# Projecting q and k as one group of seven half-size products, with sums of tokens and of weights

## The chip, the cores and the metric

The kernel runs on one core of one Trainium2 chip. The metric is the device time of one execution in microseconds (us), lower being better. Of the kernel before, three runs are shown: 1118.29 us in the median, 1117.27 to 1118.49.

## What is computed

Two layers of an encoder over 256 tokens of width 1024. Each layer has a feed-forward stage (SwiGLU of width 2816), a mixing stage, and a second feed-forward stage, with an RMS norm ahead of and behind each. The change is in the mixing stage, whose input is projected to five things:

```python
h = rms_norm(x, mix_pre_g[l])
u_pool, q_da, k_da, v_da, q_ca = jnp.split(h @ w_in[l], IN_SPLITS, axis=-1)   # 256, 512, 512, 512, 256 columns
...
q = apply_partial_rope(q_da.reshape(B, S, DA_HEADS, 2, DA_HEAD_DIM), cos, sin)
k = apply_partial_rope(k_da.reshape(B, S, DA_HEADS, 2, DA_HEAD_DIM), cos, sin)
...
kv = rms_norm(mem, mem_norm_g[l]) @ w_mem_kv[l]
...
merged = g_pool * (y_pool @ w_br_pool[l]) + g_da * (y_da @ w_br_da[l]) + g_ca * (y_ca @ w_br_ca[l])
x = x + rms_norm(merged @ w_out[l], mix_post_g[l])
```

Differential attention uses q, k and v; cross-attention uses q_ca and the keys and values that are made of 256 memory tokens; a pooling branch uses u_pool; three gates of 1024 columns each weigh the branches.

## The kernel before

**Numbers in two parts.** TensorE (PE) multiplies numbers of a reduced f32 kind. To keep precision, each operand is split into a high part (a cast on ScalarE, ACT: L119 for weights, L164 and L175 for tokens) and a low part (what is left, on VectorE, DVE: L120, L165, L176). Each product of two tiles is then three matmuls, high by high, high by low and low by high (`mm3`, L229).

**Weights.** They come packed in units of 128x2048 (`_pack`, L924), each 1 MB, in the order of use. `load_unit` (L100) loads a unit into one of five `raw` buffers; `split_unit` (L113) makes `wh` and `wl` of it, in halves of 1024 columns or, for the first five units of a stage, in quarters of 512; `wts` has five buffers of each. So loading and splitting run ahead of PE by as many units as there are buffers.

**Tokens.** The normed tokens lie turned (channels on partitions) as a pair of high and low parts, `xhl` in the profile: `xt_pair` (L170), two buffers used in turn. `pre_norm` (L187) makes them at the end of the stage ahead: it norms one half of the tokens (128 of them; index c) on DVE and ACT, turns it on PE (L207) and splits it. The turns of the second half are issued only after a given number of matmuls of the next stage (`T_UP`, by `issue_after`), so that PE has other work while the norm runs.

**The mixing stage** (`mix`, L596). Four units hold the weights of q (512 columns, upper and lower half of the 1024 input channels) and of k. For each token half c, `form_b2` (L264) makes q and then k, 24 matmuls of 512 columns each, so 96 in all; ACT copies them out of PSUM (L623), DVE rotates 16 columns of each head (L627 to L630), PE turns the result (L634) and ACT copies that (L635). Then follow v (two units, 48 matmuls), the pooled channels and q of the cross-attention (one unit each, `form_a`, 48 matmuls of 256 columns each), the memory's keys and values (48 matmuls), and the gates (288 matmuls). The scores, softmaxes and their products are strewn among these: `fill` lists the matmuls from v on, and `place(at)` issues a step after matmul number `at` of the list (`T_KT`, `T_DA`, `T_PV`, `T_SC`, `T_LN`, `T_CA`, `T_CAV`).

**Memory tokens.** `mem_gain` (L578) loads the memory's tokens in the feed-forward stage ahead (L583), and the mixing stage scales and splits them behind q and k (L637, by L175 and L176).

**Groups that are there already.** In the second feed-forward stage of both layers and the first of layer 1, three pairs of up-projection tiles are made as a group (`group`, L384): a product of 256 tokens, 1024 channels and 1024 columns in seven products of half the size each way, by a scheme of Strassen's kind. DVE makes sums of weight tiles in place on the raw units (L366, 128x2048), sums of token tiles once per stage (`token_sums`, L374, from plain copies that `pre_norm` keeps, L212), and adds the products up (L366, 128x512). `PLAN` puts downs and ups between the groups.

Which instruction stands where on an engine is set by a scheduler that lists the program engine by engine; `issue_after` adds an order by hand. Each engine takes its own list strictly in that order.

Of the kernel before, what the change touches and what calls it, by code (L numbers as in the profile page):

```python
# [9 lines left out]
F32 = mybir.dt.float32  # L10
# [24 lines left out]
T_ROPE = 13  # L35
# [5 lines left out]
T_KT = (200, 222)  # L41
# [10 lines left out]
def encoder_kernel(ctx, tc, x_d, xt_d, mem_d, memt_d, pos_d, w_d, gains_d, cols_d, lamv_d, poolw_d, cst_d, out_d):  # L52
# [6 lines left out]
    xts = ctx.enter_context(tc.tile_pool(name="xts", bufs=2))  # L59
# [110 lines left out]
    def xt_pair():  # L170
        t = xts.tile([P, 2, 2, KT, P], F32R, name="xhl")
        return t[:, 0], t[:, 1], t.rearrange("p s c k t -> p (s c) k t")
# [93 lines left out]

    def rows_chunk(c, banks, todo, lhs_of, first, last):
        done = []
        for b in range(2):
            fs = slice(b * 512, (b + 1) * 512)  # L270
            for (w, kk) in todo:
                wh = w[0].rearrange("p (k m) -> p k m", k=2)
                wl = w[1].rearrange("p (k m) -> p k m", k=2)
                for k in range(2):
                    ah, al = lhs_of(c, kk, k)
                    for i, (a, ww) in enumerate(((ah, wh), (ah, wl), (al, wh))):
                        done.append(nc.tensor.matmul(  # L277
                            out=banks[b], lhsT=a, rhs=ww[:, k, fs],
                            start=(kk == first and k == 0 and i == 0),
                            stop=(kk == last and k == 1 and i == 2),  # L280
                        ))
        return done
# [14 lines left out]
    def ffn(i, xx, late, kept, g_post, finish, ahead, raw_rstd=None):  # L297
# [53 lines left out]
        def up_both(p):  # L351
            ws = (next_unit(), next_unit())
            for c in range(2):
                up(p, c, ws, leave=1 - c)
                if kept and p == 2 and c == 0:
                    token_sums()

        def product(out, at, w, first=True, last=True):
            wv = [t.rearrange("p (k m) -> p k m", k=4) for t in w]
            return mm3(out, [(at(k), (wv[0][:, k, :], wv[1][:, k, :])) for k in range(4)], first, last)  # L360

        def tokens(c, b):
            return lambda k: (xx[0][:, c, 4 * b + k, :], xx[1][:, c, 4 * b + k, :])

        def add(out, a, b):
            nc.vector.tensor_tensor(out=out, in0=a, in1=b, op=ALU.add)  # L366

        if kept:
            sums = xts.tile([P, 2, 4 * 4, P], F32R, name="xhl")

            def summed(j):
                return lambda k: (sums[:, 0, 4 * j + k, :], sums[:, 1, 4 * j + k, :])

        def token_sums():  # L374
            a11, a12, a21, a22 = (kept[c, b] for c in range(2) for b in range(2))
            s1 = t2()
            nc.vector.tensor_tensor(out=s1, in0=a22, in1=a21, op=ALU.subtract)
            nc.vector.tensor_tensor(out=a21, in0=a11, in1=a21, op=ALU.subtract)
            nc.vector.scalar_tensor_tensor(out=a11, in0=s1, scalar=-1.0, in1=a11, op0=ALU.mult, op1=ALU.subtract)
            nc.vector.scalar_tensor_tensor(out=a12, in0=a11, scalar=-1.0, in1=a12, op0=ALU.mult, op1=ALU.subtract)  # L380
            for j, t in enumerate((s1, a11, a21, a12)):
                split(t.rearrange("p (k t) -> p k t", t=P), sums[:, 0, 4 * j:4 * j + 4, :], sums[:, 1, 4 * j:4 * j + 4, :])
# [195 lines left out]
    def mem_gain(l):  # L578
        mm = xt_pair()
        loaded = []  # L580
        for b in range(4):
            t = hids.tile([P, 2, 2, P], F32, name="hid")
            nc.sync.dma_start(out=t, in_=memt_d[:, b * 512:(b + 1) * 512].rearrange("p (k c t) -> p k c t", k=2, c=2))  # L583
            loaded.append(t)

        def scaled():
            for b, t in enumerate(loaded):
                for i in range(2):
                    k = 2 * b + i
                    col = 3 * DEPTH + KT + KT * l + k  # L590
                    gained_split((mm[0][:, :, k, :], mm[1][:, :, k, :]), t[:, i], colt[:, col:col + 1])
            return mm

        return scaled

    def mix(l, xx, late, mm, finish):  # L596
# [4 lines left out]
        qkT = wts.tile([P, 2, 2, HEADS, P], F32, name="wh")  # L601
        qT, kT = qkT[:, 0], qkT[:, 1]
# [3 lines left out]
        kc = kv[:, 1536:2048].rearrange("p (t s) -> p t s", t=2)  # L606
        held = rawp.tile([P, 2048], F32, name="raw")
        vc, up, pooled, pw = (held[:, a:b].rearrange("p (t s) -> p t s", t=2) for a, b in ((0, 512), (512, 1056), (1056, 1568), (1568, 1824)))
        nc.sync.dma_start(out=pw, in_=poolw_d[l])

        ws = [next_unit() for _ in range(4)]
        done, wait = [], []
        for c in range(2):
            qk = s4.tile([P, D], F32, name="s4")
            for p in range(2):
                ps = ma_bank()
                now = form_b2(ps, ws[2 * p], ws[2 * p + 1], c, xx)
                done += now
                if c == 0 and p == 1:
                    issue_after(late, done[T_UP])  # L620
                issue_after(wait, now[T_ROPE])
                wait = []
                nc.scalar.copy(out=qk[:, p * 512:(p + 1) * 512], in_=ps)  # L623
            g = qk.rearrange("p (g d) -> p g d", d=64)
# [6 lines left out]
            for dst, off in ((qT, 0), (kT, 512)):  # L631
                tp = mb_bank()
                for h in range(HEADS):
                    wait.append(nc.tensor.transpose(out=tp[:, h * P:(h + 1) * P], in_=qk[:, off + h * P:off + (h + 1) * P], identity=ident))  # L634
                nc.scalar.copy(out=dst[:, c], in_=tp.rearrange("p (h t) -> p h t", h=HEADS))  # L635

        mm = mm()  # L637
        ws = [next_unit() for _ in range(2)]
        fill, placed = [], []

        def place(at):
            placed.append((at, []))
            return placed[-1][1]

        for c in range(2):
            ps = ma_bank()
            now = form_b2(ps, ws[0], ws[1], c, xx)
            fill += now
            issue_after(wait, now[T_ROPE])
            wait = []  # L650
            nc.scalar.copy(out=v[:, c, :], in_=ps)

        w = next_unit()
# [78 lines left out]
        yh, yl, _ = xt_pair()  # L732
# [75 lines left out]
        mg = xt_pair()  # L808
# [45 lines left out]
    cur = xt_pair()  # L854
# [18 lines left out]
    for i, (kind, l, row) in enumerate(stages):  # L873
        nx = {}

        def finish(c):
# [5 lines left out]
            if c == 0:  # L882
                nx["xx"] = xt_pair()
                nx["kept"] = {} if stages[i + 1][0] == "ffn" else None
# [3 lines left out]
        if kind == "ffn":  # L888
            def ahead():
# [3 lines left out]
                if row == 0:  # L893
                    nx["mem"] = mem_gain(l)

            late = ffn(i, cur, late, kept, gain(l * 10 + row + 1), finish, ahead, [rst[:, c:c + 1] for c in range(2)] if i == 0 else None)
        else:
            late = mix(l, cur, late, mem, finish)
        cur, mem, kept = nx.get("xx"), nx.get("mem"), nx.get("kept")
# [24 lines left out]
def _pack(a, np):  # L924
# [34 lines left out]
    for l in range(L):  # L959
        ffn(a["ffn1_w_up"][l], a["ffn1_w_down"][l], l == 0)  # L960
        wi = a["w_in"][l]
        for s in (256, 768, 1280):
            wide(wi, slice(s, s + 512))
# [53 lines left out]
```

## Time and profile before

| | |
|---|---|
| median of 3 runs | 1118.29 us |
| the profiled execution, whole | 1117.58 us |
| its span, from the first to the last instruction | 1115.3 us |
| PE busy | 1106.0 us (99%) |
| DVE busy | 892.5 us (80%) |
| ACT busy | 652.0 us (58%) |
| granted PE clock, mean | 0.999 |

The profile gives busy time by engine, groups of instructions by line and shape (count, busy time, mean of one), what each engine waited for, and instructions in order of time from the span's start. The first mixing stage's q starts at 194.57 us, that of layer 1 at 741.47. A matmul's listed duration overlaps its neighbours'; what one costs in a row of many is the distance from start to start.

### The profile page before, as it was taken

The numbers are of one execution on the slowest core, as the hardware profiler recorded it, in microseconds if no ns is written. First come the engines' busy times: TensorE is split into PE (matmuls) and PEld (weight loads), VectorE is DVE, ScalarE is ACT, GpSimd is POOL, SyncE is SP. The second block draws the span as 40 slices with busy tenths as digits, with TensorE's granted clock in tenths as the row PEclk, the third lists the DMA queues.
The fourth block names the chain that finished last, engine by engine and source line by source line (L and its number), as shares of the span: only waits on it lengthen the run. The fifth ranks groups of instructions, "written<-read, shape, count | busy, mean of one in ns | idle before, by whom it ended". The sixth has DMA issues, their size and how long they took to land.

```text
span 1115.3 us, 13906 instructions
## 1 busy us (share of the span) xinstructions
PE 1106.0 (99%) x5247; PEld 912.4 (82%) x5247; DVE 892.5 (80%) x1215; ACT 652.0 (58%) x1082; POOL 25.0 (2%) x37
## 2 busy tenths in 40 slices
PE   9999999999999999999999999999999999999997
PEld 6888888888888888888888888888888888888886
DVE  6765556757857899999989999996676678999994
ACT  7656345646575557474675574765566647575571
POOL 0000000000000100000000000010000001000000
PEclk9999999999999999999999999999999999999999
DMA  9966543564563453563951736575445644273731
GB/s 343 385 239 227 214 150 130 189 227 144 198 218 139 173 205 132 209 244 135 332 199 71 302 118 221 201 269 196 170 172 191 236 158 175 89 254 138 286 114 38
DMA packets 35489, 218.27 MB, mean 196 GB/s; under 512 B 4192, under 2 KB 4448, under 8 KB 11232
## 3 DMA queue, kind: packets, MB, share of 16 engines
q1 hardware_dynamic: 35424, 217.40, 53.6%
q8 instruction: 41, 0.67, 0.2%
q14 instruction: 24, 0.20, 0.0%
HBM read 216.33 MB, written 1.05 MB: 195 GB/s over the span
## 4 chain that ended last, share of the span: by engine, by line
PE 97%; DMA 1%; ACT 1%; DVE 0%; POOL 0%; issue 0%; SPq 0%; DVEq 0%; POOLq 0%; ACTq 0%
PE ma L235 52%; PE acc L277 26%; PE mb L235 9%; PE acc L235 5%; PE mb L325 2%; PE mb L207 1%; PE acc L672 1%; PE acc L695 1%; PE mb L564 1%; DMA hid<-in_xt 1%; PE acc L758 1%; DMA raw<-in_w 0%; PE acc L742 0%; PE mb L831 0%; PE mb L634 0%; ACT wh L119 0%
## 5 line engine op out<-in xcount | busy, mean ns | idle before, releaser
L120 DVE TENSOR_TENSOR wl<-raw,wh 128x1024 fp32r<-128x1024 f32 (+1 forms) x498 | 524.5, 1093 | 99.2 <-ACT wh L119 96.8
L119 ACT CAST wh<-raw 128x1024 fp32r<-128x1024 f32 (+1 forms) x498 | 445.0, 949 | 198.0 <-DVE raw L366 62.1
L235 PE MATMUL ma<-wh,xhl 128*128 128x512 f32 x1664 | 529.8, 393 | 0.7 <-ACT wh L119 0.7
L235 PEld LDWEIGHTS ma<-wh,xhl 128*128 128x128 f32 x1664 | 311.5, 188 | 66.3 <-ACT wh L119 1.8
L235 PE MATMUL ma<-wl,xhl 128*128 128x512 f32 x832 | 327.0, 393 | 0.2 <-DVE wl L120 0.2
L277 PE MATMUL acc<-wh,hid 128*128 128x512 f32 x704 | 228.1, 395 | 0.0
L235 PEld LDWEIGHTS ma<-wl,xhl 128*128 128x128 f32 x832 | 156.4, 188 | 32.7 <-issue 1.0
L277 PEld LDWEIGHTS acc<-wh,hid 128*128 128x128 f32 x704 | 132.2, 188 | 27.0
L277 PE MATMUL acc<-wl,hid 128*128 128x512 f32 x352 | 136.7, 390 | 0.0
L235 PE MATMUL mb<-wh,xhl 128*128 128x512 f32 x280 | 90.4, 389 | 0.0
L366 DVE TENSOR_TENSOR raw<-raw 128x2048 f32<-128x2048 f32 x36 | 82.4, 2288 | 0.4
L277 PEld LDWEIGHTS acc<-wl,hid 128*128 128x128 f32 x352 | 66.3, 188 | 12.6
L235 PEld LDWEIGHTS mb<-wh,xhl 128*128 128x128 f32 x280 | 52.6, 188 | 10.9
L235 PE MATMUL mb<-wl,xhl 128*128 128x512 f32 x140 | 54.5, 389 | 0.0
L235 PE MATMUL acc<-wh,xhl 128*128 128x512 f32 x160 | 51.6, 391 | 0.0
L340 ACT ACTIVATE s<-ma 128x256 f32<-128x256 f32 x24 | 8.9, 386 | 64.6 <-PE ma L235 64.3
L148 POOL TENSOR_TENSOR sm<-sm,mhalf 128x1 f32<-128x1 f32 (+1 forms) x26 | 22.0, 846 | 1002.0 <-DVE sm L157 822.8
L155 ACT ACTIVATE junk<-acc 128x512 bf16<-128x512 f32 x24 | 14.4, 599 | 48.0 <-PE acc L277 48.0
L277 PE MATMUL acc<-wh,xhl 128*128 128x512 f32 x128 | 40.7, 394 | 0.0
L164 ACT CAST hid<-mb 128x256 fp32r<-128x256 f32 x88 | 32.1, 370 | 13.1 <-PE mb L325 10.3
L165 DVE TENSOR_TENSOR hid<-mb,hid 128x256 fp32r<-128x256 f32 x88 | 36.6, 419 | 1.6 <-ACT hid L164 1.4
L235 PEld LDWEIGHTS acc<-wh,xhl 128*128 128x128 f32 x160 | 30.0, 188 | 6.1
(161 smaller groups left out, 882.7 us busy)
## 6 DMA issues: line engine op xcount, KB each, us to landing
raw<-in_w SPq DMA_DIRECT2D x189, 1024.0 KB, 4.8
gain<-in_gains SPq DMA_DIRECT2D x17, 512.0 KB, 4.2
raw<-in_w SPq DMA_DIRECT2D x8, 256.0 KB, 5.6
hid<-in_memt SPq DMA_DIRECT2D x8, 256.0 KB, 7.5
hid<-in_xt SPq DMA_DIRECT2D x4, 256.0 KB, 5.3
raw<-in_w SPq DMA_DIRECT2D x2, 512.0 KB, 7.3
x<-in_x SPq DMA_DIRECT2D x4, 256.0 KB, 6.6
hid<-in_mem SPq DMA_DIRECT2D x4, 256.0 KB, 7.5
```

The source lines that it names most:

```text
L119: high = nc.scalar.copy(out=h[:, cs], in_=raw[:, cs])
L120: low = nc.vector.tensor_tensor(out=l[:, cs], in0=raw[:, cs], in1=h.bitcast(F32)[:, cs], op=ALU.subtract)
L148: nc.gpsimd.tensor_tensor(out=r, in0=v, in1=mhalf[:, :n], op=ALU.pow)
L155: sq.append(nc.scalar.activation(out=junk, in_=h, func=AF.Square, scale=fold / 32.0, accum_out=s[:, i:i + 1]))
L164: high = nc.scalar.copy(out=h, in_=ps)
L165: return high, nc.vector.tensor_tensor(out=l, in0=ps, in1=h.bitcast(F32), op=ALU.subtract)
L207: tps.append(nc.tensor.transpose(out=ps[:, k * P:(k + 1) * P], in_=xn[:, i * P:(i + 1) * P], identity=ident))
L235: done.append(nc.tensor.matmul(out=out, lhsT=lhsT, rhs=rhs, start=(first and i == 0), stop=(last and i == n - 1)))
L277: done.append(nc.tensor.matmul(out=banks[b], lhsT=a, rhs=ww[:, k, fs], start=(kk == first and k == 0 and i == 0), stop=(kk == last and k = ...
L325: nc.tensor.transpose(out=tp[:, u * P:(u + 1) * P], in_=hn[:, u * P:(u + 1) * P], identity=ident)
L366: nc.vector.tensor_tensor(out=out, in0=a, in1=b, op=ALU.add)
L564: ins.append(nc.tensor.transpose(out=tp[:, i * P:(i + 1) * P], in_=a[:, hh, kt * P:(kt + 1) * P], identity=ident))
```

## The change

q and k are made as one group. The weights of q and k are four raw units: w11 and w12 (upper half of the channels; columns of q, columns of k), w22 and w21 (lower half; k, q). The group's seven products are, in the order of the code: pa (w11), pe (w21), pd (w11+w12), pb (w11+w12+w22), pc (w12+w22), pf (w22) and pg (w21+w11+w12+w22), each 12 matmuls of 512 columns; pd, pb, pc and pf take sums of tokens. v comes first: its first token half ahead of the group, its second between pe and pd. The rotation, the turns and their copies follow behind the group, among the matmuls of the pooled channels and of q_ca (`T_ROPE` is now a pair of places in `fill`). The memory's tokens are loaded and split behind that too, in the mixing stage, no longer ahead of it. `fill` loses v's 48 matmuls, and `T_KT` is lowered by 48; the other places keep their numbers. The token pairs have two named buffers, `xa` and `xb`, in place of `xhl`. `pre_norm` keeps plain copies of the tokens ahead of every stage now (four more copies on ACT per mixing stage).

```diff
-T_ROPE = 13
+T_ROPE = (13, 40)
-T_KT = (200, 222)
+T_KT = (152, 174)
...
-        ws = [next_unit() for _ in range(4)]
-        done, wait = [], []
-        for c in range(2):
-            qk = s4.tile([P, D], F32, name="s4")
-            for p in range(2):
-                ps = ma_bank()
-                now = form_b2(ps, ws[2 * p], ws[2 * p + 1], c, xx)
...
+        ws = [next_unit() for _ in range(2)]
+        done = v_half(0)
+        w11, w12, w22, w21 = (next_raw() for _ in range(4))
+        pa, pe = ma_bank(), ma_bank()
+        done += product(pa, tokens_of(xx, 0, 0), split_unit(w11, 2))
+        nc.scalar.copy(out=u2, in_=pa)
+        done += product(pe, tokens_of(xx, 0, 1), split_unit(w21, 2))
+        add(s, u2, pe)
+        issue_after(late, done[T_UP])
+        token_sums(kept, sums)
+        v_half(1)
+        add(w11, w11, w12)
+        pd = mb_bank()
+        product(pd, summed(0), split_unit(w11, 2))
+        add(w11, w11, w22)
+        add(w12, w12, w22)
+        pb = mb_bank()
+        product(pb, summed(1), split_unit(w11, 2))
+        add(u2, u2, pb)
+        add(w21, w21, w11)
+        pc = ma_bank()
+        product(pc, summed(2), split_unit(w12, 2))
+        add(u3, u2, pc)
+        add(u2, u2, pd)
+        add(v1, u3, pd)
+        pf = mb_bank()
+        product(pf, summed(3), split_unit(w22, 2))
+        add(u2, u2, pf)
+        pg = ma_bank()
+        product(pg, tokens_of(xx, 1, 1), split_unit(w21, 2))
...
+            if c == 1:
+                add(u3, u3, pg)
...
+        mm = mem_gain(l, 1 - slot)
...
-                nx["kept"] = {} if stages[i + 1][0] == "ffn" else None
+                nx["kept"] = {}
...
-        for s in (256, 768, 1280):
-            wide(wi, slice(s, s + 512))
+        wide(wi, slice(1280, 1792))
+        for half, col in ((0, 256), (0, 768), (1, 768), (1, 256)):
+            block(wi, half, col)
```

`product` makes 12 matmuls (four channel tiles, three each), `add` is one DVE addition, `token_sums` four DVE operations of 128x512 and four splits (a cast on ACT, a subtraction on DVE). In the changed kernel's lines, additions are L275, splits still L119, L120, L164 and L165, turns of q and k L673.

What stands on DVE in the first mixing stage. Before, behind the norm of the second token half: rotations of q and k of either token half (`s4_1738`, `s4_1809`; `csd` and `snd` are cosines and sines) and splits of the units of v (`wl_1899`, `wl_1911`), of the pooled channels (`wl_1971`) and of q_ca (`wl_2031`).

```order
L627 TENSOR_TENSOR s2_1791<-s4_1738,csd_105 128x256
L628 TENSOR_TENSOR s2_1792<-s4_1738,snd_106 128x16x8
L629 TENSOR_TENSOR s2_1792<-s4_1738,snd_106 128x16x8
L630 TENSOR_TENSOR s4_1738<-s2_1791,s2_1792 128x16x16
L120 TENSOR_TENSOR wl_1899<-raw_1896,wh_1898 128x512 x4
L120 TENSOR_TENSOR wl_1911<-raw_1908,wh_1910 128x1024 x2
L627 TENSOR_TENSOR s2_1862<-s4_1809,csd_105 128x256
L628 TENSOR_TENSOR s2_1863<-s4_1809,snd_106 128x16x8
L629 TENSOR_TENSOR s2_1863<-s4_1809,snd_106 128x16x8
L630 TENSOR_TENSOR s4_1809<-s2_1862,s2_1863 128x16x16
L120 TENSOR_TENSOR wl_1971<-raw_1968,wh_1970 128x1024 x2
L120 TENSOR_TENSOR wl_2031<-raw_2028,wh_2030 128x1024 x2
```

And now at the same place. `raw_1739` is w11, `raw_1741` w12, `raw_1743` w22, `raw_1745` w21; `wl_1829` is the low part of w11+w12, `wl_1850` that of w11+w12+w22, `wl_1871` that of w12+w22; `s2` are kept tokens and their sums, `xb_1686` the split sums.

```order
L286 SCALAR_TENSOR_TENSOR s2_1585<-s2_1787,s2_1585 128x512
L120 TENSOR_TENSOR wl_1829<-raw_1739,wh_1828 128x1024
L287 SCALAR_TENSOR_TENSOR s2_1594<-s2_1585,s2_1594 128x512
L165 TENSOR_TENSOR xb_1686<-s2_1585,xb_1686 128x512
L165 TENSOR_TENSOR xb_1686<-s2_1668,xb_1686 128x512
L165 TENSOR_TENSOR xb_1686<-s2_1594,xb_1686 128x512
L120 TENSOR_TENSOR wl_1829<-raw_1739,wh_1828 128x1024
L275 TENSOR_TENSOR raw_1741<-raw_1741,raw_1743 128x2048
L275 TENSOR_TENSOR raw_1739<-raw_1739,raw_1743 128x2048
L275 TENSOR_TENSOR raw_1745<-raw_1745,raw_1739 128x2048
L120 TENSOR_TENSOR wl_1850<-raw_1739,wh_1849 128x1024 x2
L120 TENSOR_TENSOR wl_1871<-raw_1741,wh_1870 128x1024 x2
```

Between the two halves of the low part for pd stand three splits of token sums, and ahead of the first low part for pb stand three additions of 128x2048.

What stands on PE. Before, where k of the first token half (bank `ma_1765`) ends and q of the second (`ma_1810`) begins; `wh_1716` to `wl_1729` are k's weights, `wh_1692` and `wl_1693` q's.

```order
L235 MATMUL ma_1765<-wl_1729,xhl_1570 128x512
L235 MATMUL ma_1765<-wh_1728,xhl_1570 128x512
L235 MATMUL ma_1810<-wh_1692,xhl_1570 128x512
L235 MATMUL ma_1810<-wl_1693,xhl_1570 128x512
L235 MATMUL ma_1810<-wh_1692,xhl_1570 128x512 x2
```

And now, where pd (bank `mb_1827`) ends; `mb_1848` is pb and `ma_1869` pc.

```order
L235 MATMUL mb_1827<-wl_1829,xb_1686 128x512
L235 MATMUL mb_1827<-wh_1828,xb_1686 128x512
L235 MATMUL mb_1848<-wh_1849,xb_1686 128x512
L235 MATMUL ma_1869<-wh_1870,xb_1686 128x512
L235 MATMUL mb_1848<-wl_1850,xb_1686 128x512
L235 MATMUL mb_1848<-wh_1849,xb_1686 128x512 x2
```

Before, one product follows the other on weights that also served the token half ahead. Now each product has weights of its own, and pc's first matmul stands ahead of pb's second, which reads the low part `wl_1850`.

132 lines of the change are left out of this document (64 added, 68 removed).

## The prediction

> **What bounds the kernel now.** I read the page's busy times and its chain of waits first.
>
> ```profile
> span 1115.3 us, 13906 instructions
> PE 1106.0 (99%) x5247; PEld 912.4 (82%) x5247; DVE 892.5 (80%) x1215; ACT 652.0 (58%) x1082; POOL 25.0 (2%) x37
> PE 97%; DMA 1%; ACT 1%; DVE 0%; POOL 0%; issue 0%; SPq 0%; DVEq 0%; POOLq 0%; ACTq 0%
> ```
>
> PE works in 99% of the span, and 97% of the chain that ended last is its own. So a matmul less is worth its whole issue time, if its operands are there, and any wait that PE gets anew is paid in full. Then the waits of PE alone (engine, tile, line, what it waited for: us in total, times, longest).
>
> ```profile
> PE acc L869 <- DVE s L866: 1.2, 1, 1.2
> PE ma L235 <- ACT wh L119: 0.7, 1, 0.7
> PE mb L712 <- DVE s L708: 0.4, 2, 0.2
> PE mb L325 <- DVE s L338: 0.4, 1, 0.4
> PE ma L235 <- DVE wl L120: 0.2, 1, 0.2
> ```
>
> That is 2.9 us, most of it at the start. There is nothing to win in waits, only in work. What a matmul costs and where a group begins stand in the chain (start, length, what), the first mixing stage in PE's own rows in order of time (its first matmul, the turns of the second token half, its first scores); then the busy times by stretch, the first mixing stage from the end of its second norm to its first scores, and a group of seven products in a feed-forward stage.
>
> ```profile
> 48.21 10.92 PE ma L235 x48
> 424.90 2.75 PE ma L235 x12
> ```
> ```profile
> 194.57 0.39 PE L235 MATMUL ma<-wh,xhl 128*128 128x512 f32 x1
> 202.97 1.03 PE L207 MATMUL mb<-ident,s 128*128 128x128 f32 x8
> 203.76 0.48 PE L235 MATMUL ma<-wl,xhl 128*128 128x512 f32 x1
> 241.50 2.00 PE L672 MATMUL acc<-wh 64*128 64x256 f32 x16
> ```
> ```profile
> core 0: us, PE busy (x) PEld busy (x) DVE busy (x) ACT busy (x) POOL busy (x), PEclk, DMA share, GB/s
> 202.10:243.40 41.30, 41.30 (x248) 36.21 (x246) 27.43 (x41) 22.16 (x31) 0.00 (x0) 1.00 0.59 210
> 424.90:447.20 22.30, 22.30 (x102) 18.44 (x101) 21.16 (x23) 18.32 (x23) 0.00 (x0) 1.00 0.51 187
> ```
>
> One matmul of 512 columns costs 10.92/48 = 0.2275 us; eight turns cost 203.76 - 202.97 = 0.79. In the mixing stage's 41.30 us DVE has 41.30 - 27.43 = 13.9 us to spare; in the group's 22.30 it has 1.1.
>
> **The change, part by part.**
>
> *PE's work.* q and k were 96 matmuls, the group has 84: 12 x 0.2275 = 2.73 us less per mixing stage, 5.46 in both. Turns, rotations and v are as many as before.
>
> *DVE's work.* These rows give its prices: groups first (busy, mean ns of one), then pieces in order of time.
>
> ```profile
> L366 DVE TENSOR_TENSOR raw<-raw 128x2048 f32<-128x2048 f32 x36 | 82.4, 2288 | 0.4
> L119 ACT CAST wh<-raw 128x1024 fp32r<-128x1024 f32 (+1 forms) x498 | 445.0, 949 | 198.0 <-DVE raw L366 62.1 <-PE ma L235 54.4 <-issue 29.7
> L212 ACT COPY s<-mb 128x512 f32<-128x512 f32 x12 | 6.7, 589 | 3.8 <-DVE xhl L165 3.8
> ```
> ```profile
> 201.21 0.88 DVE L199 TENSOR_SCALAR s<-s,sm 128x512 f32<-128x512 f32 x2 [0.44 <-POOL sm L148]
> 220.15 4.63 DVE L120 TENSOR_TENSOR wl<-raw,wh 128x1024 fp32r<-128x1024 f32 x4
> 410.82 2.29 DVE L366 TENSOR_TENSOR raw<-raw 128x2048 f32<-128x2048 f32 x1
> 413.03 1.22 DVE L120 TENSOR_TENSOR wl<-raw,wh 128x1024 fp32r<-128x1024 f32 x1
> 418.10 0.69 DVE L379 SCALAR_TENSOR_TENSOR s<-s,s 128x512 f32<-128x512 f32 x1
> 418.70 0.69 DVE L165 TENSOR_TENSOR xhl<-s,xhl 128x512 fp32r<-128x512 f32 x1
> 422.25 2.28 DVE L366 TENSOR_TENSOR raw<-raw 128x2048 f32<-128x2048 f32 x1
> ```
>
> From start to start, half a unit's low part takes about 1.135 us (four end after 4.63, the last alone being 1.22), an addition of 128x2048 413.03 - 410.82 = 2.21, anything of 128x512 0.60. q and k had four units to split, the group has seven: 6 x 1.135 = 6.8 us more. Four wide additions: 8.8. Token sums: four operations and four splits, 4.8. Seven additions of products: 4.2. Together 24.6 us per mixing stage, where 13.9 were to spare. So 10.7 us don't fit, and by the balance alone PE would wait about that long. The memory's eight scalings only change place.
>
> *The walk.* The order of the instructions says where. Behind the second norm (L199, which ends at 202.1) DVE has, up to the low half that pb's second matmul reads: seven halves (two each of w11, w21 and w11+w12, one of w11+w12+w22), 7.95 us; four wide additions, 8.84; eleven pieces of 128x512 (two splits of the turned tokens, the four sums and four splits, one addition of a product), 6.60. Together 23.4. ACT keeps two plain copies of the first token half ahead of the square that starts the second norm (about 0.5 us each), while four quarter splits leave DVE's list there, so I let the norm end 0.3 later, at 202.4 (between 202.1 and 203.1). The low half is then ready at 225.8.
>
> PE starts at 194.57 and has ahead of that matmul 86 others (v's 48, pa, pe and pd with 36, the first of pb and of pc) and eight turns: 19.57 + 0.79, so it could be there at 214.9. It stands idle for 10.9 us in all on the way: at the turns and at w11's and w21's low parts, in the middle of pd, most of it between pd and pb. Then DVE has seven halves more and five additions of products up to the last half of pg's weights, 7.95 + 3.0 = 10.95, to 236.75; PE has 41 matmuls, 9.33, to 235.1. It waits 1.6 again. Together 12.5 us idle, against 2.73 saved: +9.8.
>
> *ACT* gets in the same stretch three units more (5.7 by the cast's mean), four casts of sums and four copies (8 x about 0.55): 22.16 + 10.1 = 32 of 41 us busy. It hides beside DVE; the high parts for pb wait for DVE's additions like the low ones. *Loads.* The group holds four of five raw units until DVE has read them, so the pooled channels' unit can only be loaded from about 227.
>
> ```profile
> raw<-in_w SPq DMA_DIRECT2D x189, 1024.0 KB, 4.8
> hid<-in_memt SPq DMA_DIRECT2D x8, 256.0 KB, 7.5
> ```
>
> It lands 4.8 later, at 231.8, and is cast by 232.9; PE wants it behind pg's first matmuls at about 235. Landing as late as the memory's tokens (7.5) would cost some 0.5; I put nothing. The memory's loads on SP move from the feed-forward stage to behind the group, where their matmuls come over 48 x 2 matmuls later.
>
> *Places of the later steps.* Since `fill` begins 48 matmuls later, the scores and softmaxes come 48 x 0.2275 = 10.9 us later among the gates; the last product has 432 - 402 = 30 matmuls (6.8 us) behind it, not 78. That still covers the split that follows. One wait each at a rotation's copy and at a score, of the sort that stands above as L712 with 0.2, may come: I put 0.5 per stage, between 0 and 1.5.
>
> *Sum:* 12.5 + 0.5 - 2.73 = +10.3 per stage, +20.6 in both. Bounds: with the norm at 202.1 and no late waits 9.5; with the norm at 203.1 and 1.5, 12.0. The profiled execution took 1117.58 us (2.28 around its span), so 1138.2; the median of the runs lies 0.7 above it, so 1139.
>
> *The clock.* Idle PE may also lose its clock. At the program's end (last matmul, then the stretches with their granted clock), and at its start:
>
> ```profile
> 1108.69 0.39 PE L277 MATMUL acc<-wh,hid 128*128 128x512 f32 x1
> 1111.00:1112.00 1.00, 0.00 (x0) 0.00 (x0) 1.00 (x2) 0.00 (x0) 0.00 (x0) 0.98 0.00 0
> 1112.00:1113.00 1.00, 0.00 (x0) 0.00 (x0) 0.26 (x1) 0.00 (x0) 0.00 (x0) 0.50 0.56 209
> 1.19 4.88 PE L869 MATMUL acc<-s 128*128 128x512 bf16 x11 [1.19 <-DVE s L866]
> ```
>
> The clock was halved just before 1112.0, 2.9 us after the last matmul's end at 1109.08; and the first eleven matmuls cost 4.88/11 = 0.44 each, twice the later price. Between pd and pb the walk has a gap: pd's last six matmuls run from 218.0 (DVE's first 15.6 us) to 219.4; two wide additions later, at 222.4, ACT may cast, and pb's first matmul runs at 223.5. That is 4.1 us with none, then one, then about 2 more. By the end's row that suffices. The Trainium skill, "TensorE: Matmul & The Clock Gate", section "Part 1: The HAM clock gate", says that the clock is halved after an idle window of about 3.4 us and restored after a busy one, in windows that run free of the program: an estimate by it is 3.4 us at half speed, 1.7 lost per stage. The trace's 2.9 us at its end agrees with free windows as far as one case can. What rows alone give is the second rival.
>
> **The rivals.**
>
> *Half covered.* The scheduler's list is right but DVE runs ahead more than I think; half of the 12.5 is hidden: 6.25 - 2.73 = 3.5 per stage, 1125. Against it: DVE is in one list, and nothing in it can pass the norm.
>
> *The clock falls too.* With 4.88 us at half speed, as at the start, PE loses 2.4 per stage, of which the 1.6 of the second wait may hide a part: 0.8 to 2.4, I take 1.7. Then +24, 1142. It decides whether the gap holds no busy stretch for as long as at the end.
>
> *Faster.* The group costs no waits, as in the feed-forward stage, where PE is busy for all 22.30 us: 1118.3 - 5.5 = 1113. For it: the same seven products. Against it: there the wide additions run at 410.82 and 422.25, up to 14 us ahead of the group's first product at 424.90, under downs and ups; here v's 10.9 us lie ahead, and DVE has the norm to do. The point: DVE's 23.4 us would have to start by 191.5, when the tokens aren't normed.
>
> *About even.* PE idles just 2.7 per stage, a quarter of the walk: 1118. Nothing speaks for it but the walk's error.
>
> **How the numbers follow.** The walk alone 0.50 (1139), with the clock 0.33 (1142), half covered 0.09, even 0.03, faster 0.05. A measurement can tell about 0.2% (2.2 us). So faster 0.05, same 0.03, slower 0.92. The range: down from 1136 (two times 9.5) towards the half-covered case, to 1131, since a few prices are taken from other stages; up to 1145, the clock's case with its dearer end (2 x (10.3 + 2.4) = 25.4, 1144).
>
> **What would show it.** Right: PE waits for DVE's low parts and ACT's high parts of L120 and L119 in the mixing stages, some 13 us in each, the longest single one of about 4 ahead of pb; PE's matmuls 24 fewer; DVE without a gap from 202 to 237; most of the first scores 10 us later than 241.5; feed-forward stages as long as before. With the clock: granted 0.5 somewhere in 222 to 231, and matmuls of 0.45. Wrong: PE waits of under 5 us per stage, or waits named by loads, or the end of the mixing stage giving back what its start lost.

## The result, and the profile after

The changed kernel takes 1143.07 us in the median of four runs (1142.2 to 1143.54), the kernel before 1117.78 (1117.26 to 1118.49) on the same chip: a ratio of 1.0226, 95% interval 1.0209 to 1.0242. It is slower by 25.3 us. The forecast was 1139, with 1142 for the case in which the clock falls too; the clock fell. The execution profiled took 1143.54, with a span of 1141.5.

First the page's span, its busy times and the shares of the chain that ended last, then the waits of PE alone.

```profile
span 1141.5 us, 13944 instructions
PE 1113.4 (98%) x5223; PEld 912.2 (80%) x5223; DVE 940.3 (82%) x1265; ACT 668.6 (59%) x1104; POOL 24.3 (2%) x37
PE 90%; DVE 4%; ACT 4%; DMA 1%; issue 1%; POOL 1%; SPq 0%; DVEq 0%; POOLq 0%; ACTq 0%
```
```profile
PE mb L235 <- ACT wh L119: 8.1, 2, 4.0
PE ma L235 <- ACT wh L119: 3.2, 3, 1.1
PE ma L235 <- DVE wl L120: 2.9, 7, 0.7
PE mb L235 <- DVE wl L120: 2.9, 2, 1.5
```

PE has 24 matmuls less (5247 to 5223), and yet is busy for 7.4 us more: some of them got dearer. DVE's busy time grew by 47.8 us, 23.9 per mixing stage, where 24.6 were reckoned. PE's share of the chain fell from 97% to 90%, DVE and ACT now have 4% each, and the waits name the high and low parts of split weights.

How much a mixing stage grew is read from one line of code: L227, which adds what a stage gave to x at its end, with its first and last start from 190 to 420 us; the last one ends the first mixing stage. The first row is the kernel before, the second the changed one.

```profile
L227 DVE SCALAR_TENSOR_TENSOR x<-s,sm,x x6: 746/748/753, 196.8 to 387.1; 128x512 f32<-128x512 f32 x6
```
```profile
L227 DVE SCALAR_TENSOR_TENSOR x<-s,sm,x x6: 746/748/753, 198.0 to 400.4; 128x512 f32<-128x512 f32 x6
```

The stage's end came 13.3 us later, and 0.4 of that stood already when its first matmul began (194.57 before, 195.00 now): 12.9 against a forecast of 10.3, or 12.0 with the clock. The mixing stage of layer 1 grew by as much: from its first matmul to the first that writes an `acc` bank from the branches' tokens it took 147.55 us before and takes 160.45 now (147.49 and 160.38 in layer 0). What lies between that matmul and the next mixing stage took 399.41 us in either kernel, so the feed-forward stages stayed as long as they were.

Where it went is seen in PE's own rows of the first mixing stage, in order of time (start, us, what; in brackets the wait ahead of it).

```profile
201.28 0.50 PE L235 MATMUL ma<-wh,xa 128*128 128x512 f32 x1 [0.45 <-ACT wl L611]
202.20 1.06 PE L207 MATMUL mb<-ident,s 128*128 128x128 f32 x8 [0.42 <-DVE s L199]
203.63 0.50 PE L235 MATMUL ma<-wl,xa 128*128 128x512 f32 x1 [0.37 <-DVE wl L120]
205.97 0.50 PE L235 MATMUL ma<-wl,xa 128*128 128x512 f32 x1 [0.67 <-DVE wl L120]
218.39 0.50 PE L235 MATMUL mb<-wl,xb 128*128 128x512 f32 x1 [1.47 <-DVE wl L120]
219.43 0.40 PE L235 MATMUL mb<-wh,xb 128*128 128x512 f32 x1
223.87 0.79 PE L235 MATMUL mb<-wh,xb 128*128 128x512 f32 x1 [4.05 <-ACT wh L119]
225.76 0.79 PE L235 MATMUL ma<-wh,xb 128*128 128x512 f32 x1 [1.10 <-ACT wh L119]
226.36 0.69 PE L235 MATMUL mb<-wl,xb 128*128 128x512 f32 x1
226.85 1.05 PE L235 MATMUL mb<-wh,xb 128*128 128x512 f32 x2
227.71 0.63 PE L235 MATMUL mb<-wl,xb 128*128 128x512 f32 x1
231.54 0.80 PE L235 MATMUL ma<-wh,xb 128*128 128x512 f32 x2
239.03 0.50 PE L235 MATMUL ma<-wl,xa 128*128 128x512 f32 x1 [0.34 <-DVE wl L120]
```

pb's first matmul is the one at 223.87, its second the one at 226.36. The waits up to there sum to 8.5. What they cost is more, since PE starts anew behind each: from start to start, 219.43 to 223.87 is 4.44 us for a matmul of 0.2275. Counted so, the eight places up to 226.36 (the seven waits, and 226.36 itself) lose 10.7 us.

From 226.36 to 231.54 PE doesn't wait, but two matmuls take 0.86 (226.85 to 227.71), so one takes 0.43 and not 0.2275. Twelve matmuls lose 5.18 - 12 x 0.2275 = 2.45 us there. The granted clock in stretches of 2 us says when (length, then busy times; the third number from the end is PEclk):

```profile
220.00:222.00 2.00, 0.00 (x0) 0.00 (x0) 2.00 (x2) 0.00 (x0) 0.00 (x0) 0.92 0.00 0
...
230.00:232.00 2.00, 2.00 (x7) 1.53 (x6) 0.64 (x2) 0.45 (x1) 0.00 (x0) 0.52 0.99 406
```

0.92 means 0.3 of the 2 us at half speed, at its end, since the stretch ahead reads 1.00, so the clock fell at about 221.7; 0.52 means that it came back at about 231.9. It was halved for 10.2 us, though PE had work without a pause from 226.36 on.

Last, DVE's rows of the same stretch.

```profile
201.57 0.88 DVE L199 TENSOR_SCALAR s<-s,sm 128x512 f32<-128x512 f32 x2
...
218.25 6.82 DVE L275 TENSOR_TENSOR raw<-raw 128x2048 f32<-128x2048 f32 x3
224.98 4.62 DVE L120 TENSOR_TENSOR wl<-raw,wh 128x1024 fp32r<-128x1024 f32 x4
231.36 0.69 DVE L275 TENSOR_TENSOR s<-s,mb 128x512 f32<-128x512 f32 x1 [1.75 <-PE mb L235]
```

The norm ends at 201.57 + 0.88 = 202.45 (forecast 202.4). Three wide additions stand in a row from 218.25; the low part for pb's second matmul is the first of the four from 224.98. Then comes what the walk did not have: DVE itself pauses for 1.75 us. Its next entry adds pb's product, which PE makes at half speed, and everything behind that entry waits with it.

### The profile page after: what moved, and what is told of

The parts are those of the page before. It is cut to its first block, busy times and chain, and to the rows that moved or that the text cites. A ratio compares the mean times of both kernels' runs of the same rounds, so it can differ in the third digit from the quotient of the medians.

```text
span 1141.5 us, 13944 instructions
## 1 busy us (share of the span) xinstructions
PE 1113.4 (98%) x5223; PEld 912.2 (80%) x5223; DVE 940.3 (82%) x1265; ACT 668.6 (59%) x1104; POOL 24.3 (2%) x37
## 4 chain that ended last, share of the span: by engine, by line
PE 90%; DVE 4%; ACT 4%; DMA 1%; issue 1%; POOL 1%; SPq 0%; DVEq 0%; POOLq 0%; ACTq 0%
PE ma L235 46%; PE acc L301 24%; PE mb L235 9%; PE acc L235 4%; PE mb L349 2%; ACT wh L119 2%; DVE wl L120 1%; PE acc L695 1%; DVE raw L275 1%; PE acc L718 1%; PE mb L568 1%; DMA hid<-in_xt 1%; PE acc L781 1%; ACT junk L155 1%; DMA raw<-in_w 0%
## 5 line engine op out<-in xcount | busy, mean ns | idle before, releaser
L120 DVE TENSOR_TENSOR wl<-raw,wh 128x1024 fp32r<-128x1024 f32 (+1 forms) x510 | 537.5, 1095 | 76.4 <-ACT wh L119 71.9
L119 ACT CAST wh<-raw 128x1024 fp32r<-128x1024 f32 (+1 forms) x510 | 455.0, 950 | 219.2 <-DVE raw L275 87.2
L235 PE MATMUL ma<-wh,xa 128*128 128x512 f32 x872 | 279.7, 394 | 2.6 <-ACT wh L119 2.1
L235 PE MATMUL ma<-wh,xb 128*128 128x512 f32 x728 | 235.0, 394 | 1.5 <-ACT wh L119 1.1
L235 PEld LDWEIGHTS ma<-wh,xa 128*128 128x128 f32 x872 | 163.8, 188 | 38.3 <-ACT wh L119 4.0
L235 PE MATMUL ma<-wl,xa 128*128 128x512 f32 x436 | 171.9, 394 | 1.6 <-DVE wl L120 1.6
L235 PEld LDWEIGHTS ma<-wh,xb 128*128 128x128 f32 x728 | 136.8, 188 | 30.7 <-ACT wh L119 1.9
L235 PE MATMUL ma<-wl,xb 128*128 128x512 f32 x364 | 143.5, 394 | 1.3 <-DVE wl L120 1.3
L275 DVE TENSOR_TENSOR raw<-raw 128x2048 f32<-128x2048 f32 x44 | 100.5, 2288 | 0.5
L235 PEld LDWEIGHTS ma<-wl,xa 128*128 128x128 f32 x436 | 82.1, 188 | 20.4 <-DVE wl L120 3.8
L235 PEld LDWEIGHTS ma<-wl,xb 128*128 128x128 f32 x364 | 68.6, 188 | 16.2 <-DVE wl L120 2.2
L235 PE MATMUL mb<-wh,xa 128*128 128x512 f32 x200 | 66.7, 400 | 4.0 <-ACT wh L119 4.0
L235 PE MATMUL mb<-wh,xb 128*128 128x512 f32 x128 | 43.5, 406 | 4.0 <-ACT wh L119 4.0
```

The source lines that it names most:

```text
L119: high = nc.scalar.copy(out=h[:, cs], in_=raw[:, cs])
L120: low = nc.vector.tensor_tensor(out=l[:, cs], in0=raw[:, cs], in1=h.bitcast(F32)[:, cs], op=ALU.subtract)
L235: done.append(nc.tensor.matmul(out=out, lhsT=lhsT, rhs=rhs, start=(first and i == 0), stop=(last and i == n - 1)))
```

## The experiments

Eight kernels, in two sets of four; each set has its own runs of the kernel before (1117.37 and 1117.52 in the median). "Over before" is the median less that.

| run | median us | over before | ratio, 95% interval |
|---|---|---|---|
| the change | 1143.07 | 25.3 | 1.0226, 1.0209 to 1.0242 |
| e1, gap filled with 16 | 1143.03 | 25.7 | 1.0223, 1.0209 to 1.0237 |
| e2, no wide sums | 1122.15 | 4.8 | 1.0041, 1.0027 to 1.0054 |
| e3, order alone | 1124.71 | 7.3 | 1.0064, 1.0051 to 1.0076 |
| e4, two sums on GpSimd | 1150.52 | 33.2 | 1.0295, 1.0281 to 1.0309 |
| e5, all gaps filled | 1140.95 | 23.4 | 1.0205, 1.0191 to 1.0219 |
| e6, cover | 1132.98 | 15.5 | 1.0140, 1.0126 to 1.0153 |
| e7, places | 1141.78 | 24.3 | 1.0216, 1.0202 to 1.0230 |
| e8, order, low parts early | 1121.93 | 4.4 | 1.0039, 1.0027 to 1.0052 |

The theory ahead of them was the prediction's: PE waits for DVE's list, which grew by more than the stage had to spare, and loses its clock in the gap. The rivals: the order (v ahead) costs the time, not the group; ACT or the loads come next as soon as DVE is quicker; the clock costs nothing, or all of the rest.

**e1: the gap between pd and pb filled.**

```diff
-        product(pd, summed(0), split_unit(w11, 2))
+        before = product(pd, summed(0), split_unit(w11, 2))
+        extra = acc_bank()
+        dummy = [nc.tensor.matmul(out=extra, lhsT=xx[0][:, 0, 0, :], rhs=xx[0][:, 0, 0:4, :], start=True, stop=True) for _ in range(16)]
+        issue_after(dummy, before[-1])
...
-        product(pb, summed(1), split_unit(w11, 2))
+        first = product(pb, summed(1), split_unit(w11, 2))
+        issue_after(first, dummy[-1])
```

> Sixteen more matmuls of 512 columns (16 x 0.2275 = 3.64 us) into a free bank, queued between pd's last and pb's first matmul in both mixing stages, so that PE is not idle for 4.05 us there; nothing else is changed, and DVE's list is the same. Theory (PE waits for DVE's list, and on top of that the halved clock takes time): in the changed kernel about 12 matmuls from 226.36 to 231.54 us cost some 0.43 in place of 0.2275, 2.4 us; of these 1.3 were idle anyway by the walk (the second wait of 1.6 came out at 0.34). So 1.1 us per mixing stage come back, 1143.1 - 2.2 = 1141 (1139.5 to 1142), granted clock 1.00 in both mixing stages, and the second wait back at 1 to 1.6. Rival 1 (the clock's 2.4 us come on top in full): 1138.3. Rival 2 (PE would have waited all the same): 1143, within 0.5.

Measured: 1143.03, as the second rival had it. But the clock had not stayed. PE's rows, and two of the stretches of 2 us:

```profile
219.31 3.79 PE L631 MATMUL acc<-xa 128*128 128x512 f32 x16
...
225.42 0.79 PE L235 MATMUL ma<-wh,xb 128*128 128x512 f32 x1 [1.39 <-ACT wh L119]
226.50 1.05 PE L235 MATMUL mb<-wh,xb 128*128 128x512 f32 x2
236.79 0.50 PE L235 MATMUL ma<-wl,xa 128*128 128x512 f32 x1 [0.90 <-DVE wl L120]
```
```profile
224.00:226.00 2.00, 0.61 (x2) 0.38 (x2) 2.00 (x3) 2.00 (x3) 0.00 (x0) 0.86 0.00 0
228.00:230.00 2.00, 2.00 (x8) 1.60 (x8) 1.26 (x2) 2.00 (x3) 0.00 (x0) 0.79 0.88 295
```

By the same reading as above the clock fell at 225.4 and came back at 228.8: 3.4 us, in place of 10.2, and no wait ahead of it was over 1.4 us (0.43 ahead of pb's first matmul at 223.53, 1.39 behind it). What PE won there it waited for later, in part at pg's low part (0.90, where it was 0.34). The theory's condition, a full clock, was not met, so e1 could not tell it from the second rival. e5 was made for that.

**e2: the wide sums left out.** The four additions of weights are left out, so q and k are other numbers; all else stays.

```diff
-        add(w11, w11, w12)
...
-        add(w11, w11, w22)
-        add(w12, w12, w22)
...
-        add(w21, w21, w11)
```

> The four additions of 128x2048 on weights are left out in both mixing stages (the products then take w11, w11, w12 and w21 as they are, so q and k are not what the reference has); all matmuls, splits, token sums and additions of products stay. Theory (DVE's list bounds the stretch): DVE loses 4 x 2.21 = 8.84 us per stage, of which 6.6 lie ahead of pb's second matmul; PE's idle time falls by 8.8, and the clock's 1.1 goes with the long gap: 1143.1 - 2 x 9.9 = 1123 (1120 to 1126), longest wait under 2 us. Rival 1 (ACT's casts end last as soon as DVE is quicker): the waits stay at 5 or more per stage, 1130 or above. Rival 2 (the wait is for the order of v, turns and norm, not for the sums): under 4 us less per stage, 1135 or above.

Measured: 1122.15, where 1123 was expected. The waits named pb and its high part are gone; PE's two largest groups of waits are now these:

```profile
PE ma L235 <- DVE wl L120: 2.9, 7, 0.7
PE ma L235 <- ACT wl L611: 1.7, 2, 0.9
```

20.5 us less over before, 10.2 per stage: the 8.84 of the additions themselves, the clock, and 0.4 more. So DVE's list was the bound, and no wait for ACT's casts or for loads took its place. What is left, 4.8, is still slower than the kernel before, with 5.5 us fewer matmuls: something else costs some 10.

**e3: the order alone.** v ahead and memory behind, but q and k as 96 plain matmuls.

```diff
-        w11, w12, w22, w21 = (next_raw() for _ in range(4))
...
-        product(pg, tokens_of(xx, 1, 1), split_unit(w21, 2))
+        wq = [next_unit() for _ in range(2)]
...
+        done += part(0, 0)
         issue_after(late, done[T_UP])
...
         v_half(1)
...
+        part(0, 1)
+        wq = [next_unit() for _ in range(2)]
+        for c in range(2):
+            part(1, c)
```

> v ahead of q and k, and memory's tokens loaded and split behind them, as in the changed kernel, but q and k as 96 plain matmuls per stage with four units split in two halves: no group, no token sums, no kept copies, no sums of weights. Theory of the prediction (order and places cost nothing; all of the time is the group's): 1117.8, within 2. Rival (in the changed kernel PE already waits 1.9 us per stage at four places from 201.3 to 206.6, ahead of any sum of weights, because v's second unit is split behind the norm): 2 x 1.9 more, 1121.6 (1120 to 1124).

Measured: 1124.71, 7.3 over before, more than even the rival gave. The order costs 3.7 per mixing stage. Two rows of it, PE's wait and DVE's list:

```profile
202.95 0.50 PE L235 MATMUL ma<-wl,xa 128*128 128x512 f32 x1 [1.72 <-DVE wl L120]
```
```profile
201.42 0.88 DVE L199 TENSOR_SCALAR s<-s,sm 128x512 f32<-128x512 f32 x2
202.21 4.90 DVE L120 TENSOR_TENSOR wl<-raw,wh 128x512 fp32r<-128x512 f32 x8
```

The low parts that PE wants behind v's first half stand behind the second norm in DVE's list.

**e4: two of the sums on GpSimd.**

```diff
-        add(w12, w12, w22)
+        nc.gpsimd.tensor_tensor(out=w12, in0=w12, in1=w22, op=ALU.add)
...
-        add(w21, w21, w11)
+        nc.gpsimd.tensor_tensor(out=w21, in0=w21, in1=w11, op=ALU.add)
```

> Two of the four additions of 128x2048 (w12 + w22 and w21 + w11) issued by GpSimd instead of DVE; GpSimd is busy for 2% of the span. Theory (DVE's list bounds the stretch): DVE loses 2 x 2.21 = 4.4 us per stage, and the gap ahead of pb gets 4.4 shorter at the place where the clock fell: 1143.1 - 2 x (4.4 + 1.1) = 1132 (1129 to 1135), so long as GpSimd takes no more than about 8 us for one. Rival 1 (GpSimd takes over 10 us for such an addition, pc or pg waits for it): no gain or slower, 1142 to 1155. Rival 2 (DVE's own operations become slower while GpSimd works beside it): 1135 to 1142, with DVE's additions and low parts longer than 2.21 and 1.135 in the rows.

Measured: 1150.52, 7.9 further over before than the change. GpSimd took 4.6 us for an addition, well under the 8 allowed, so the first rival's reason doesn't hold. GpSimd's rows, then DVE's:

```profile
210.63 4.62 POOL L631 TENSOR_TENSOR raw<-raw 128x2048 f32<-128x2048 f32 x1 [9.61 <-DVE raw L275]
224.14 4.52 POOL L635 TENSOR_TENSOR raw<-raw 128x2048 f32<-128x2048 f32 x1 [8.89 <-DVE raw L275]
```
```profile
210.47 0.69 DVE L275 TENSOR_TENSOR s<-s,ma 128x512 f32<-128x512 f32 x1
211.06 4.74 DVE L285 TENSOR_TENSOR s<-s,s 128x512 f32<-128x512 f32 x1
225.12 8.04 DVE L120 TENSOR_TENSOR wl<-raw,wh 128x1024 fp32r<-128x1024 f32 x4 [1.11 <-ACT wh L119]
```

A subtraction of 0.69 took 4.74: it began at 211.06, while GpSimd's addition ran to 215.25, and ended at 215.80, 0.55 behind it. Four low parts took 8.04 in place of 4.62. DVE lost 4.05 + 3.42 = 7.5 us to GpSimd and was relieved of 4.4, so 3.1 per stage, about 6 of the 7.9, are named; for the rest no run was made. This is the second rival's effect, much larger than it put it: not slower operations, but one that stands still. The operation at 210.47, which has one input in a bank of products, ran on at 0.69 while GpSimd began at 210.63. The Trainium skill, "SBUF — State Buffer", section "Who interferes with whom", says that a DVE instruction with two inputs in SBUF contends with one of GpSimd that reads SBUF, and that one with at most one such input does not, outside the modes that use two ports. All three rows of DVE agree with it.

**e5: all gaps filled.** Six more matmuls in the middle of pd, eighteen behind it, seven behind pb's first.

`filler(n, early)` queues n matmuls of 512 columns into a free bank behind `early` and gives the last of them.

```diff
+        md = product(pd, summed(0), split_unit(w11, 2))
+        issue_after(md[7:], filler(6, md[6]))
+        last = filler(18, md[-1])
...
+        mb = product(pb, summed(1), split_unit(w11, 2))
+        issue_after(mb, last)
+        last = filler(7, mb[0])
+        issue_after(mb[1:], last)
```

> As the run with sixteen filling matmuls, but in all three gaps around pb: six in the middle of pd (ahead of its eighth matmul), eighteen between pd and pb, seven between pb's first and second (31 x 0.2275 = 7.1 us per stage, all into a free bank, in time that was idle). With sixteen the clock still fell for 2.6 us and the time stayed at 1143.0. Theory (DVE's list sets the time, but the list itself paused 1.75 us in the changed kernel and 1.49 with sixteen, because its addition of pb's product stands ahead of the next low parts and PE made pb at half speed): at full clock these pauses go, 1.2 per stage: 1140.6 (1139.5 to 1141.8), granted clock 1.00 all through. Rival (what the clock loses PE would have waited anyway, all of it): 1143, within 0.7, with the second wait, at pg's low part, grown to 2 or more.

Measured: 1140.95, the theory's 1140.6, not the rival's 1143. One stretch of those in which the clock was halved in the changed kernel, then DVE's entry that adds pb's product with the two later ones at which it paused:

```profile
226.00:228.00 2.00, 2.00 (x9) 1.28 (x8) 2.00 (x3) 2.00 (x4) 0.00 (x0) 1.00 0.04 8
```
```profile
229.96 0.68 DVE L275 TENSOR_TENSOR s<-s,mb 128x512 f32<-128x512 f32 x1
232.01 0.69 DVE L275 TENSOR_TENSOR s<-s,ma 128x512 f32<-128x512 f32 x1 [0.24 <-PE ma L235]
236.62 0.69 DVE L275 TENSOR_TENSOR s<-s,mb 128x512 f32<-128x512 f32 x1 [0.46 <-PE mb L235]
```

The clock stays at 1.00, and DVE pauses for 0.7 in place of 1.75. The clock's share of the change is 1.9 to 2.1 us, about 1.0 per stage. The two stages of the profiled executions differ: fourteen of the sixteen first scores start 59.44 and 59.47 us behind their stage's first matmul in the changed kernel, 58.48 and 57.99 in e5, so 0.96 and 1.48 earlier. In the first stage of e5 PE also waited 1.08 for a load that landed later (the row stands further down), in the second it did not. So the clock cost 1.0 to 1.5 per stage; the rest of the 2.45 that its matmuls lose would have been waits.

**e6: more of PE's work ahead of the sums.** The units of the pooled channels and of cross-attention's q go between v's second half and pe, pe goes behind them, and one pair of gate units goes ahead of memory's keys and values; the later places are lowered to fit.

```diff
+        wpool, wqc = (next_raw() for _ in range(2))
+        w11, w21, w12, w22 = (next_raw() for _ in range(4))
...
         v_half(1)
+            fill += form_a(ps[:, t * S:(t + 1) * S], w, slice(t * P, (t + 1) * P), xx)
...
+            fill += form_a(ps[:, t * S:(t + 1) * S], w2, slice(t * P, (t + 1) * P), xx)
...
+        product(pe, tokens_of(xx, 0, 1), split_unit(w21, 2))
```

> The group with more of PE's work ahead of its sums: behind both halves of v come the pooled channels' and cross-attention's q units (96 matmuls of 256 columns, 11.3 us at 0.118), then the product of w21, then the six products that need sums; one pair of gate units goes ahead of memory's keys and values; the later places are lowered to fit. DVE's list gets four halves earlier (4.5 us), its total is the same. Theory (what is lost is the wait for a list that starts when the norm ends, and cover ahead of it hides it): the 8.0 us lost between 207 and 226 in the changed kernel become 1.2, of which 2 to 3 come back behind the group, where rotations, memory's scalings and the gates' low parts are now late, and the clock stays: 1143.0 - 2 x 5.5 = 1132 (1128 to 1136). Rival 1 (DVE has no room in the whole stretch up to 260, the order doesn't matter): 1141 to 1144, the waits only move. Rival 2 (cover hides everything): 1126 or less.

Measured: 1132.98, where 1132 was expected: 9.8 of the 25.3 are covered. Its stretches show what is won and what comes back (length, PE busy, and so on), and below them stand its first wait and a stretch behind that:

```profile
207.00:226.00 19.00, 18.89 (x129) 17.43 (x128) 18.33 (x21) 9.86 (x15) 0.00 (x0) 0.97 0.19 63
240.00:262.00 22.00, 18.88 (x96) 14.71 (x95) 21.96 (x47) 19.24 (x38) 0.00 (x0) 1.00 0.49 182
```
```profile
203.40 0.50 PE L235 MATMUL ma<-wl,xa 128*128 128x512 f32 x1 [2.79 <-DVE wl L120]
```
```profile
206.00:208.00 2.00, 2.00 (x8) 1.61 (x8) 1.88 (x2) 0.59 (x1) 0.00 (x0) 0.50 0.31 41
```

In the changed kernel PE was busy for 12.38 of the first stretch and 21.82 of the second. The wait ahead of pb is gone; 2.9 us of it stand behind the group, where DVE works 21.96 of 22 us. The first wait for a low part behind the norm, 0.37 in the changed kernel (at 203.63), grew to 2.79, since pe's first matmul and the turns no longer fill it. And the clock did not stay, as the theory had it: it was halved from about 204.8 to 208.2, and as long in the second mixing stage. The cover ahead of pb works, but it left a hole at the norm.

**e7: the later places lowered by 48**, in the six tables behind the first softmax.

```diff
-T_SC = (242, 336)
+T_SC = (194, 288)
...
-T_CAV = (391, 402)
+T_CAV = (343, 354)
```

> The changed kernel with the places of scores, turns, products and norms behind the first softmax (six tables) lowered by 48, so that they stand as far from the end of the gates as before the change. Theory (late places cost the waits that the trace names, 0.2 to 0.4 per stage): 1142.4, within 0.8. Rival 1 (all of the 1.0 us that a stage loses from 262 to 300 hangs on these places): 1141 or less. Rival 2 (lowered, they meet softmaxes that aren't done): 1144 or more.

Measured: 1141.78, 1.0 less over before than the change. That lies within what was expected of the theory and just above the first rival's bound; the intervals of the two kernels overlap widely. The places are worth about 0.5 per stage by the medians, which the noise does not separate from nothing.

**e8: the order alone, with two low parts ahead of the norm's last operations** in DVE's list (beside e3's edit; the line numbers of this kernel are a little higher).

```diff
+        for low in lows[-4:-2]:
+            issue_after(norm_ops[0:], low)
+        done += part(0, 0)
```

> The order alone (v ahead, memory behind, q and k plain), with one thing changed: the first two quarter low parts of the second weight pair stand ahead of the second norm's last operations in DVE's list, where the list was idle, not behind them. Theory (the order's price is the wait of 1.72 us for that low part, and so the place in DVE's list): 1124.7 - 2 x 1.3 = 1122.1 (1121 to 1123.2), and no wait over 1 us at the start of the mixing stages. Rival (the price lies in the later places and in memory's scalings behind the rotations): 1124.7, within 0.6.

Measured: 1121.93, as the theory had it: 2.9 of the order's 7.3 us go. DVE's rows at that place:

```profile
199.34 3.69 DVE L122 TENSOR_TENSOR wl<-raw,wh 128x512 fp32r<-128x512 f32 x6
202.95 1.29 DVE L197 TENSOR_TENSOR s<-x,gain 128x512 f32<-128x512 f32 x2
```

Six low parts are done by 203.03, and the wait of 1.72 is gone. The norm pays for them by coming later, yet the kernel gains. No run takes the other 4.4 us of the order, 2.2 per stage, apart, but PE's rows place most of them. The first matmul behind the sixteen first scores comes 50.69 us after the stage's first one, against 48.86 in the kernel before, so 1.8 later. Up to there one wait is named, 0.33 at the norm's turns. The scores, before in one row of 1.93 us (from 241.50 to 243.43), stand in three pieces of 0.63, 0.63 and 1.49, with other matmuls between.

No version here beats the kernel before: the best one with a full group, e6, is 15.5 us over it.

## Why the prediction was right, and what it missed

**The verdict and its mechanism** held: slower, inside the range, because PE waits for DVE's list. e2 shows it by taking entries out of the list, e6 by putting PE's work ahead of it.

**PE's saving** of 2.73 per stage is there in the count of matmuls; of time nothing is left of it in the changed kernel.

**The walk to pb's second matmul** was right in its end and its sum: 225.8 forecast, 226.36 found; 10.9 idle forecast, 10.7 lost. It put them at the turns, at w11's and w21's low parts, in the middle of pd, and most between pd and pb, and there they are, but for the first: at 201.28 PE waits 0.45 for ACT's copy of v out of its bank, which the walk did not have. This could be walked because DVE works its list in order and each entry had a row. That it met the norm's end to 0.05 was luck: the 0.3 that it allowed for the plain copies did not come (the norm ends 7.45 us behind the stage's first matmul, 7.52 before the change), and this execution's stage happened to begin 0.43 later. DVE's list took some 23.8 us, not 23.4.

**The second wait** of 1.6 came out at 0.34, with 2.45 lost to the slow clock just ahead of it.

**The step that failed** is the weight given to the clock. The prediction showed a gap of 4.1 us with no matmul, said of it "By the end's row that suffices", and still gave the case without the clock 0.50 and the case with it 0.33. Its own row, taken at its word, should have made the second the likeliest: 1142, against 1143.07. But that row was one case: at the ends of the ten kernels profiled here the clock fell 2.0 (e1) to 5.0 us (e6) after the last matmul. And the prediction read it wrongly where it says that its 2.9 us agree with windows of 3.4 us: a window of that length that is idle throughout does not fit between the last matmul and the fall. What the falls in the mixing stages have in common is how little PE had to do in the 3.4 us ahead; the last section has the numbers. The price of 1.7 per stage (0.8 to 2.4) was a little too high by e5, which gives 1.0 to 1.5.

**Almost 3 us more were missed.** Without the clock (e5) the change is 23.4 over before, against 20.6 forecast: 1.4 per stage. The 0.5 for late waits was too small, and the bound named for it was 1.5. Some of it is seen in PE's rows of the changed kernel: two of the sixteen first scores run from 248.11, behind a wait of 0.18, to 248.74, the other fourteen from 254.44 to 256.37, where all sixteen took 1.93 in a row before; that is about 0.8 more. The later places give 0.5 back in e7, within the noise. And the pooled channels' unit, put at nothing, can cost. Its load was forecast to land at 231.8 and is split from 232.23 in the changed kernel; in the first mixing stage of e5 it is split from 234.25, and PE waits for that:

```profile
234.25 2.19 ACT L119 CAST wh<-raw 128x512 fp32r<-128x512 f32 x4 [3.34 <-DMA raw<-in_w]
```
```profile
234.92 0.51 PE L235 MATMUL ma<-xa,wh 128*128 128x256 f32 x2 [1.08 <-ACT wh L119]
```

In the second mixing stage of e5 PE does not wait for it. The rest of the 1.4 stays open.

**The order** was taken as free, apart from that 0.5: v's matmuls are as many as before. e3 prices it at 3.7 per stage with no group there. The walk had part of this in its idle times at the turns and low parts, which is why its sum came out right all the same; but it charged them to the group. Of the 25.3 us, 7.3 are the order's; taking the wide sums out of the changed kernel gives 20.5 back, the clock among them; and what remains of the group, with its fewer matmuls, its token sums and its additions of products, saves 2.5 (4.8 against 7.3). These are differences between kernels taken in one order, and parts that share a wait could come out otherwise in another.

**The rivals.** "Half covered", "about even" and "faster" all needed DVE to be ahead of its list; it is busy for 18.79 of the 19 us from 207 to 226:

```profile
207.00:226.00 19.00, 12.38 (x51) 9.21 (x49) 18.79 (x18) 8.58 (x12) 0.00 (x0) 0.89 0.00 0
```

## What to carry to other kernels

A trick that trades matmuls for additions needs room on the adding engine ahead of the first product that takes a sum; here that room was missing. Walk its list from the last thing that holds it (here a norm) to that product, and compare with what the matrix engine has to do meanwhile. When a step is moved ahead, look at what stands in front of its operands in the other engines' lists: equal work in another order cost 7.3 us. And the wait of 4 us on the matrix engine cost more than itself, since the matmuls behind it ran at half speed and held up the engine that waited for their product.

## What the runs showed of the hardware

**The clock can fall without a long gap.** In e1 no wait was over 1.4 us, and yet the clock was halved at about 225.4. In the 3.4 us ahead of that PE had some five matmuls to do, 1.1 us of work; in the changed kernel, ahead of 221.7, five as well. From 214.9 to 218.3 there, with some eight matmuls in 3.4 us, it kept its clock. In all, the clock fell once in each mixing stage of the changed kernel, e1, e4, e6 and e7, and each time three to six matmuls had started in the 3.4 us ahead. The longest wait alone does not decide: in e4's second mixing stage PE waited 3.09 us (up to 782.05, with no matmul begun in the 3.4 us ahead) and kept its clock, in e6 it waited 2.79 (up to 203.40) and lost it. So it also matters where such lengths of time begin.

**The slow stretches come in multiples of 3.4 us.** The ten slow stretches were 3.4 us long (e1 and e6), 10.2 (the changed kernel, e7, and e4's second) or 17.1 (e4's first): one, three and five times the same length. If they are cut into lengths of 3.4 from their start, the clock stayed low behind one in which PE was busy for 2.78 us (217.56 to 220.97 in e4), and came back behind one with 3.01 (757.8 to 761.2 in e6). The Trainium skill, "TensorE: Matmul & The Clock Gate", section "Part 1: The HAM clock gate", has windows of about 3.4 us that run free of the program, which agrees with these lengths; it speaks of an idle window, and here one that was a third busy was enough.

**A DVE operation with two inputs in SBUF stood still while GpSimd added two tiles in SBUF**: 0.69 us became 4.74 (e4). One with an input in a PSUM bank took 0.69 beside the same addition.
